# The heads' norm without reciprocals, the last combination in PSUM, the first keys queued ahead of the values' projection, the mLSTM's first loads off the queue of stores

## The chip, the core and the metric

The kernel runs on one core of a Trainium2 chip. The core has five engines that run side by side, each through its own list of instructions in order: PE (TensorE, matmuls and transposes), DVE (VectorE), ACT (ScalarE), POOL (GpSimd) and SP (SyncE, which issues most DMAs). The metric is the device time of one execution, in microseconds (us). The kernel before took 3703.52 us (median of three runs, 3697.98 to 3706.41).

## The reference

Two layers of a diffusion backbone over 1024 latent tokens and 256 context tokens, width 1024. A layer normalizes, projects, mixes by three groups of heads (a long convolution "hyena", an mLSTM, differential attention), projects back (`w_out`), routes each token to two of 32 experts, and adds up. What the change touches, cut:

```python
def diff_core(q, k, v, lam):                    # 4 heads, two maps m of 64 each
    s = einsum('bqhmd,bkhmd->bhmqk', q, k) * 64 ** -0.5
    pr = softmax(s, axis=-1)
    a = pr[:, :, 0] - lam * pr[:, :, 1]
    return einsum('bhqk,bkhe->bqhe', a, v)      # 128 wide

y_da = rmsnorm(o, da_subln_w) * (1 - lam_init)  # norm of each head's 128
rmsnorm(x, w) = x * rsqrt(mean(x * x) + 1e-6) * w
y = concat([y_hy, y_ml, y_da]) @ w_out          # x = x + g1 * y, norm, router
f = gate_0 * expert_0(h) + gate_1 * expert_1(h) # two experts per token
out = rmsnorm(x + g2 * f, final_norm_w)         # after the last layer
```

In layer 1 only the latent tokens are computed to the end; in layer 0 the 256 context tokens also attend, among themselves.

## The kernel before

Everything runs in stages, and each layer has the same ones: projections and hyena (with `da_v`, the projection of the attention's values, woven in; L329 stores them to `vD`), attention, the output stage `wout` (into which `ml_out`, the mLSTM's output, is woven), the experts. After layer 1's experts stands `final`.

**Attention** (`attention`, L1036 on) goes over 16 pairs of head and block of 256 queries, and in layer 0 over one more, the context (`None`). Its instructions stand on PE, DVE, ACT and POOL in an order that is written by hand: `AT_ORDER` (L1240) lists the steps of one iteration, in which pair i is scored, pair i-1 transposed and pair i-2 multiplied by the values. With x the half of 128 queries and m the map: `Sxm` are six matmuls of scores into one of two PSUM tiles `at_sc` (L1107); `Mxm` DVE's maximum over 1280 scores (L1113); `Exm` ACT's exponential, which also gives the row's sum (L1122); `Cx` (`comb`, L1127) makes c = -lambda * sum0 / sum1 on DVE (L1130, L1131), the reciprocal R = 1 / sum0 (L1132), and on POOL E1 * c (L1134) and E0 + E1 (L1138); `T`, `U`, `L` transpose on PE, copy the high part on ACT (L1161) and subtract for the low part on DVE (L1166). `O` and `Q` step the generator `out1` (L1169): value matmuls `at_av`, copy and square on ACT, the sum of squares by a matmul (`at_st`), then on DVE two multiplications by R (L1188, L1189), the mean (`rs_v`, L186), on POOL the power -1/2 (`rs_r`, L188), on DVE r * R (L1192), on PE its transpose `at_rb` (L1196), on DVE the product (L1198), on SP the store (L1199). `W` lets POOL round one piece of `w_out` (L1254). SP isn't in the hand-written order: a scheduler places its DMAs, each of which waits in line for those ahead of it, for its buffer, and for an earlier DMA of its ring of eight.

Queries have two buffers `at_q`, keys six `at_k` (four of them one head's). The context's queries lie in two `at_k`. The loads of an iteration stand in `prep` (L1044).

**The start of wout**: `ml_out(l, i)` loads five tiles for block i of 128 tokens (L925 to L932; in layer 0 the first two blocks from ACT's queue, the others from SP's) and computes `m_s` (scores), `m_o`, `m_i`, `m_p` on PE with exponentials and products between; `wout` (L1265) loads router weights `wr`, norm weights, `wo_x` and `wo_y` (the mixed heads), and multiplies `wo_o` by `w_out`. The router weights arrive with 4 and 32 numbers in a row of `wr`.

**The end**: `combine` (L1849) and `final` (L1891) take eight tiles of 128x1024: ACT gate0 * y0 (L1866), DVE + gate1 * y1 (L1867), POOL * g2 (L1868), DVE + x (L1869), ACT square and sum (L1900), DVE and POOL the inverse root, DVE x * r * w (L1902), store.

Of the kernel before, what the change touches and what calls it, by code (L numbers as in the profile page):

```python
# [8 lines left out]
F32 = mybir.dt.float32  # L9
# [20 lines left out]
class Kern:  # L30
# [885 lines left out]
    def ml_out(self, l, i, p, ps, psb):  # L916
# [6 lines left out]
        q = nc.scalar if i < 2 and l == 0 else nc.sync  # L923
# [112 lines left out]
    def attention(self, l, cx, p, pk, ps, psc, fill):  # L1036
# [5 lines left out]

        def prep(i):

            ctx = pairs[i] is None
            kt = lambda: pk.tile([128, 1280], F32R, name="at_k", bufs=6)
            vt = lambda: pk.tile([128, 10, 128], F32R, name="at_v", bufs=4)
            if ctx:
                kd = [[kt()[:, 0:1024].rearrange("p (h t) -> p h t", h=4) for y in range(2)] for m in range(2)]
# [11 lines left out]
                q = [kt()[:, 0:1024].rearrange("p (m h t) -> p m h t", m=2, h=4) for _ in range(2)]  # L1061
                for qi in range(2):
                    for m in range(2):
                        c = SEQ + qi * 128
                        for y in range(2):
                            nc.sync.dma_start(q[qi][64 * y:64 * y + 64, m].bitcast(F32),
                                              self.qkD[l][0, :, y, 64 * m:64 * m + 64, c:c + 128]
                                              .rearrange("h d t -> d h t"))
            else:
                h, qb = pairs[i]  # L1070
                q = pk.tile([128, 2, 256], F32R, name="at_q", bufs=2)
                for y in range(2):
                    nc.sync.dma_start(q[64 * y:64 * y + 64].bitcast(F32), self.qkD[l][0, h, y, :, qb * 256:(qb + 1) * 256]
                                      .rearrange("(m d) t -> d m t", m=2))
                if qb == 0:
                    kd = [[kt() for y in range(2)] for m in range(2)]
                    for m in range(2):
                        for y in range(2):
                            for x in range(2):
                                nc.sync.dma_start(kd[m][y][64 * x:64 * x + 64, :].bitcast(F32),  # L1080
                                                  self.qkD[l][1, h, y, 64 * m:64 * m + 64])
# [11 lines left out]

        def smm(i, x, m):
            u = st[i]
            w = u["nk"] * 128
            sc = u["sc"][x][m] = psc.tile([128, 1280], F32, name="at_sc", bufs=2)
            if u["ctx"]:
                for h in range(4):
# [1102 lines left out]
```

## Time and profile before

| | |
|---|---|
| time, three runs | 3697.98, 3703.52, 3706.41 us |
| the profiled execution: its own time, its span | 3701.92 us, 3700.1 us |
| mean granted TensorE clock | 0.924 of 2.4 GHz |
| busy: PE, DVE, ACT, POOL | 3214.9, 2553.5, 1726.5, 1175.7 us |
| layer 0: attention starts, ends | about 709, 978 us |
| layer 1: attention starts, ends | about 2543, 2801 us |
| the final combination | about 3643 to 3697 us |

The engines' busy shares (PE 87%, DVE 69%, ACT 47%, POOL 32%) are means over stages with different limits. A view of groups gives, for one line of the program, its instructions' total and mean; the idle time behind it is what the engine waited ahead of them and what ended the wait. In a view of a stretch in time, rows are in order and carry the idle time before them in brackets. A queue of DMAs ("SPq", "ACTq") shows when each issue began and how long it held the queue.

### The profile page before, as it was taken

How to read it: one execution, taken by the hardware profiler on the slowest of the kernel's cores; microseconds unless marked ns; L12 is line 12 of the kernel's file. 1: busy time of each engine (PE TensorE's matmuls, PEld its weight loads, DVE VectorE, ACT ScalarE, POOL GpSimd, SP SyncE). 2: the span in 40 equal slices, each digit the busy share in tenths (PEclk: the TensorE clock that was granted, in tenths of full speed). 3: DMA queues.
4: the chain of work that ended last, by engine and by line, in shares of the span. 5: the costliest groups of instructions: out<-in, count | busy, mean ns of one | idle time of the engine just before them, and what ended most of it. 6: DMA issues, size and time to landing. Idle time of an engine off the chain costs nothing. (4 is left out here: it accounts for less than half of the span.)

```text
span 3700.1 us, 48647 instructions
## 1 busy us (share of the span) xinstructions
PE 3214.9 (87%) x16486; PEld 2565.4 (69%) x16486; DVE 2553.5 (69%) x4367; ACT 1726.5 (47%) x2685; POOL 1175.7 (32%) x1101
## 2 busy tenths in 40 slices
PE   5999899888598898999997798987887989999992
PEld 2666777777577676677775687786776867777672
DVE  5444577488487687767676835875884877877776
ACT  3323233366332265556565423333663245666663
POOL 4000444277453212222110702442774411111104
PEclk7999899999798899999999799998998989999996
DMA  6889676543555677979797735776424578999985
GB/s 216 274 276 333 171 208 198 165 117 92 153 187 186 239 270 254 368 275 382 294 359 277 246 93 177 221 218 181 119 69 150 175 294 294 374 358 344 344 327 204
DMA packets 388509, 877.16 MB, mean 237 GB/s; under 512 B 60766, under 2 KB 244585, under 8 KB 332193
## 3 DMA queue, kind: packets, MB, share of 16 engines
q1 hardware_dynamic: 328945, 644.13, 51.8%
q10 hardware_dynamic: 25103, 145.74, 10.9%
q0 software_dynamic: 34208, 84.14, 7.2%
q8 instruction: 132, 2.16, 0.2%
q14 instruction: 121, 0.98, 0.1%
HBM read 750.32 MB, written 154.77 MB: 245 GB/s over the span
## 5 line engine op out<-in xcount | busy, mean ns | idle before, releaser
L1619 DVE TENSOR_TENSOR e_lo<-e_raw,e_hi 128x1024 fp32r<-128x1024 f32 x632 | 758.0, 1223 | 176.7 <-ACT e_hi L1618 168.4
L1618 ACT CAST e_hi<-e_raw 128x1024 fp32r<-128x1024 f32 x632 | 648.6, 1050 | 236.4 <-PE e_h L70 138.3
L68 PE MATMUL e_h<-e_hi,e_xh 128*128 128x512 f32 x768 | 328.8, 430 | 8.3 <-ACT e_hi L1618 8.2
L69 PE MATMUL e_h<-e_lo,e_xh 128*128 128x512 f32 x768 | 314.2, 409 | 2.3 <-DVE e_lo L1619 2.2
L70 PE MATMUL e_h<-e_hi,e_xl 128*128 128x512 f32 x768 | 300.9, 393 | 0.0
L68 PE MATMUL p_u<-hT,u_w 128*128 128x512 f32 (+1 forms) x768 | 290.7, 379 | 3.5 <-ACT u_w L60 3.5
L69 PE MATMUL p_u<-hT,u_w 128*128 128x512 f32 (+1 forms) x768 | 287.9, 375 | 0.0
L70 PE MATMUL p_u<-hT,u_w 128*128 128x512 f32 (+1 forms) x768 | 285.6, 373 | 0.0
L1600 PE MATMUL e_h<-e_raw,e_xf 128*128 128x512 f32 x512 | 249.6, 609 | 2.4 <-DVE e_sl L1611 2.2
L1653 POOL DMA_INDIRECT yD<-e_yo,rt_idx x66 | 88.3, 1338 | 479.2 <-ACT e_hi L1618 338.5
L1565 POOL DMA_INDIRECT e_xg<-h2D,rt_idx x66 | 84.2, 1276 | 488.3 <-PE e_tr L1581 352.6
L1122 ACT ACTIVATE at_e<-at_sc,at_S 128x1280 f32<-128x1280 f32 (+1 forms) x144 | 177.6, 1237 | 97.4 <-DVE at_S L1113 88.9
L1107 PE MATMUL at_sc<-at_k,at_q 128*128 128x512 f32 (+1 forms) x768 | 193.0, 388 | 32.2 <-DMA at_k<-qkD 23.5
L1113 DVE TENSOR_REDUCE at_S<-at_sc 128x1 f32<-128x1280 f32 (+1 forms) x132 | 194.1, 1472 | 33.7 <-PE at_sc L1107 28.6
L69 PE MATMUL e_y<-e_lo,e_hh 128*128 128x512 f32 x512 | 208.0, 410 | 1.4 <-DVE e_lo L1619 1.2
L70 PE MATMUL e_y<-e_hi,e_hl 128*128 128x512 f32 x512 | 193.0, 394 | 1.9 <-DVE e_hl L61 1.9
L1138 POOL TENSOR_TENSOR at_e<-at_e,at_e 128x1280 f32<-128x1280 f32 (+1 forms) x66 | 192.1, 2910 | 5.5
L68 PE MATMUL e_y<-e_hi,e_hh 128*128 128x512 f32 x512 | 181.6, 407 | 10.4 <-ACT e_hi L1618 8.0
L1107 PEld LDWEIGHTS at_sc<-at_k,at_q 128*128 128x128 f32 x768 | 143.1, 200 | 61.8 <-issue 23.3
L68 PEld LDWEIGHTS e_h<-e_hi,e_xh 128*128 128x128 f32 x768 | 145.2, 189 | 51.7 <-ACT e_hi L1618 17.8
L69 PEld LDWEIGHTS e_h<-e_lo,e_xh 128*128 128x128 f32 x768 | 145.0, 189 | 43.8 <-issue 11.4
L68 PEld LDWEIGHTS p_u<-hT,u_w 128*128 128x128 f32 x768 | 148.3, 193 | 35.6 <-issue 7.0
(576 smaller groups left out, 8287.9 us busy)
## 6 DMA issues: line engine op xcount, KB each, us to landing
e_raw<-in_moe_w_dram SPq DMA_DIRECT2D x259, 1024.0 KB
e_raw<-in_moe_w_dram ACTq DMA_DIRECT2D x121, 1024.0 KB
adaw<-in_ada_w_dram SPq DMA_DIRECT2D x48, 1024.0 KB
at_k<-qkD SPq DMA_DIRECT2D x64, 320.0 KB
u_raw<-in_w_in_dram SPq DMA_DIRECT2D x36, 512.0 KB
cb_y<-yD SPq DMA_DIRECT2D x36, 512.0 KB
hW<-in_c_hw_dram POOLq DMA_DIRECT2D x32, 512.0 KB, 4.9
at_v<-vD SPq DMA_DIRECT2D x16, 640.0 KB
```

The lines of the kernel that those rows point to most:

```text
L68: mm(out, L[0], R[0], start=start, stop=False)
L69: mm(out, L[0], R[1], start=False, stop=False)
L70: mm(out, L[1], R[0], start=False, stop=stop)
L1107: nc.tensor.matmul(sc[:, c:c + n], u["q"][:, m, x * 128:(x + 1) * 128], u["kd"][m][y][:, c:c + n], start=(y == 0), stop=(y == 1))
L1113: nc.vector.tensor_reduce(u["S"][x][:, m, 0:u["nh"]], sc[:, 0:w].rearrange("p (h t) -> p h t", h=u["nh"]), axis=AX.X, op=OP.max, negate=True)
L1122: nc.scalar.activation(e[:, cs], u["sc"][x][m][:, cs], AF.Exp, bias=S[:, m, h:h + 1], accum_out=S[:, 2 + m, h:h + 1])
L1138: nc.gpsimd.tensor_tensor(E[0], E[0], E[1], op=OP.add)
L1565: self.nc.gpsimd.indirect_dma_start(out=xg, out_offset=None, in_=self.h2D[l][0:NT, :], in_offset=bass.IndirectOffsetOnAxis(ap=gi, axis=0), ...
L1600: nc.tensor.matmul(hp[x], xx[0][:, k, :], raw[:, cs], start=(k == 0), stop=False)
L1618: self.nc.scalar.copy(hi, raw)
L1619: self.nc.vector.tensor_tensor(lo, raw, hi.bitcast(F32), op=OP.subtract)
L1653: u["o"].append(nc.gpsimd.indirect_dma_start(out=self.yD[l][0:2 * NT, :], out_offset=bass.IndirectOffsetOnAxis(ap=s, axis=0), in_=y, in_of ...
```

## The change

Six edits.

1. R is no longer a reciprocal. As E0 + E1 * c isn't divided by sum0, the norm can take EPS * sum0^2 in the place of EPS. `comb` computes that for both halves in one DVE instruction at C1 (L1149 of after) and drops both reciprocals; `out1` makes o / 128 + R in one instruction (L1205), POOL takes the power from it, and PE transposes that power directly: r * R (L1192) is gone, and one `Q` step.
2. `final` has its own loop: ACT writes gate0 * y0 into PSUM, three DVE instructions work there (+ gate1 * y1, * g2, + x), ACT squares from there; for six tiles ACT multiplies by r and POOL by w, for the last two DVE does both.
3. Queries have four buffers, and the context's queries lie in these, each loaded for itself ahead of its keys.
4. `first()` puts the first queries and keys ahead of those tiles of `da_v` that are emitted after hyena has ended (its memory is then free).
5. The mLSTM's loads all go by SP's queue; the attention's last two pairs store by POOL's queue; the exponentials `at_e` have a pool of their own, which is given back apart from the rest.
6. The router weights go through two contiguous tiles, and two DVE copies per layer.

```diff
@@ ml_out
-        q = nc.scalar if i < 2 and l == 0 else nc.sync
+        q = nc.sync
@@ attention: prep
+                q = [[qt().rearrange("p m (a t) -> p (m a) t", a=2) for m in range(2)] for _ in range(2)]
...
-                q = [kt()[:, 0:1024].rearrange("p (m h t) -> p m h t", m=2, h=4) for _ in range(2)]
-                q = pk.tile([128, 2, 256], F32R, name="at_q", bufs=2)
+                q = self.at_first[0] if i == 0 else self.at_queries(l, pk, h, qb)
                 if qb == 0:
-                    kd = [[kt() for y in range(2)] for m in range(2)]
+                    kd = self.at_first[1] if i == 0 else self.at_keys(l, pk, h)
@@ attention: comb, out1
             nc.vector.reciprocal(c, S[:, 3, 0:n])
             nc.vector.scalar_tensor_tensor(c, S[:, 2, 0:n], nlam, c, op0=OP.mult, op1=OP.mult)
-            nc.vector.reciprocal(u["R"][:, 0:n, x], S[:, 2, 0:n])
+            if x == 1:
+                s = u["S"][:, :, 2, 0:n].rearrange("p x h -> p h x")
+                nc.vector.scalar_tensor_tensor(u["R"][:, 0:n, :], s, EPS, s, op0=OP.mult, op1=OP.mult)
...
-            nc.vector.tensor_tensor(t, o[:, 0:2], R, op=OP.mult)
-            nc.vector.tensor_tensor(t, t, R, op=OP.mult)
-            r = self.rstd(p, t, 2, 1.0 / 128)
-            yield
-            nc.vector.tensor_tensor(R, r, R, op=OP.mult)
+            nc.vector.scalar_tensor_tensor(t, o[:, 0:2], 1.0 / 128, R, op0=OP.mult, op1=OP.add)
+            r = p.tile([128, 2], F32, name="rs_r", bufs=3)
+            nc.gpsimd.tensor_tensor(r, t, self.nhalf.to_broadcast([128, 2]), op=OP.pow)
...
-                nc.tensor.transpose(o[:, x * 128:(x + 1) * 128], R[:, x:x + 1].to_broadcast([128, 128]), self.ident)
+                nc.tensor.transpose(o[:, x * 128:(x + 1) * 128], r[:, x:x + 1].to_broadcast([128, 128]), self.ident)
...
-            nc.sync.dma_start(self.yTD[l][4 + h, :, u["qb"] * 256:(u["qb"] + 1) * 256], ob)
+            (nc.gpsimd if u["last"] else nc.sync).dma_start(self.yTD[l][4 + h, :, u["qb"] * 256:(u["qb"] + 1) * 256], ob)
...
-    AT_ORDER = """S00 O M00 T0 S01 T1 U0 O L0 E00 Q Q U1 M01 S10 T2 L1 E01 T3 O Q S11 U2 C0 O T4 M10 U3 E10 L2 L3
+    AT_ORDER = """S00 O M00 T0 S01 T1 U0 O L0 E00 Q U1 M01 S10 T2 L1 E01 T3 O Q S11 U2 C0 O T4 M10 U3 E10 L2 L3
@@ wout
+            wg = p.tile([128, 8, 4], F32, name="wr_g", tag="wo_h", bufs=2)
+            we = p.tile([128, 8, 32], F32, name="wr_e", tag="wo_h", bufs=2)
...
+            nc.vector.tensor_copy(wr[:, :, 0:4], wg)
+            nc.vector.tensor_copy(wr[:, :, 4:36], we)
@@ final
+                t = ps.tile([128, D], F32, name="fin_t", bufs=4)
+                nc.scalar.mul(t, y[0], self.gate[:, i, 0:1])
+                nc.vector.scalar_tensor_tensor(t, y[1], self.gate[:, i, 1:2], t, op0=OP.mult, op1=OP.add)
+                nc.vector.tensor_tensor(t, t, g2, op=OP.mult)
+                nc.vector.tensor_tensor(t, t, xt, op=OP.add)
+                nc.scalar.activation(sq, t, AF.Square, accum_out=ss)
+                r = self.rstd(p, ss, 1, 1.0 / D)
+                if i < 6:
+                    nc.scalar.mul(sq, t, r)
+                    nc.gpsimd.tensor_tensor(sq, sq, fw, op=OP.mult)
+                else:
+                    nc.vector.scalar_tensor_tensor(sq, t, r, fw, op0=OP.mult, op1=OP.mult)
@@ the layer
+                    def first():
+                        self.pk = cb.enter_context(pool(f"akv{l}", **right))
+                        self.at_first = self.at_queries(l, self.pk, 0, 0), self.at_keys(l, self.pk, 0)
...
                             with pool(f"wv{l}") as pw:
+                                if self.hyd:
+                                    first()
                                 yield from self.da_v(l, hT, pw)
...
+                pe = cb.enter_context(pool(f"ate{l}"))
```

DVE in a middle iteration of layer 0's attention, first before, from the sum of squares of one pair (`at_ms`) over C1 and M00 to the second subtraction; `at_A` are the subtractions L4, L0 and L1, `at_S` what belongs to the scores:

```order
L1188 TENSOR_TENSOR at_ms<-at_st,at_R 128x2
L1189 TENSOR_TENSOR at_ms<-at_ms,at_R 128x2
L186 TENSOR_SCALAR rs_v<-at_ms 128x2
L1166 TENSOR_TENSOR at_A_7598<-at_t,at_A_7597 128x512
L1130 RECIPROCAL at_S_7572<-at_S_7572 128x1
L1131 SCALAR_TENSOR_TENSOR at_S_7572<-at_S_7572,at_nl 128x1
L1132 RECIPROCAL at_R<-at_S_7572 128x1
L1113 TENSOR_REDUCE at_S_7719<-at_sc 128x1
L1166 TENSOR_TENSOR at_A_7746<-at_t,at_A_7745 128x4x128
L1192 TENSOR_TENSOR at_R<-rs_r,at_R 128x2
L1113 TENSOR_REDUCE at_S_7719<-at_sc 128x1
```

The same place on DVE of after:

```order
L1205 SCALAR_TENSOR_TENSOR at_ms<-at_st,at_R 128x2
L1183 TENSOR_TENSOR at_A_7555<-at_t,at_A_7554 128x512
L1145 RECIPROCAL at_S<-at_S 128x1
L1146 SCALAR_TENSOR_TENSOR at_S<-at_S,at_nl 128x1
L1149 SCALAR_TENSOR_TENSOR at_R<-at_S 128x2
L1128 TENSOR_REDUCE at_S<-at_sc 128x1
L1183 TENSOR_TENSOR at_A_7697<-at_t,at_A_7696 128x4x128
L1128 TENSOR_REDUCE at_S<-at_sc 128x1
```

Between the subtraction L0 and the maximum M01 nothing stands any more, three instructions for the mean are one, and behind C1's c stands the new product of the sums.

SP (the queue of loads and stores) at the end of layer 1's attention, before; `at_o` are the attention's stores, `ml_` the mLSTM's first block:

```order
L1199 DMA yTD_100<-at_o 128x256
L1252 DMA wo_raw<-in_w_out_dram 128x512
L1199 DMA yTD_100<-at_o 128x256 x3
L925 DMA ml_v<-vmD_90 128x260
L927 DMA ml_Cs<-CsD_98 128x260
L930 DMA ml_Mb<-mD_86 128x512 x2
L932 DMA ml_qk<-mqkD_92 128x4x128
```

The same place on SP of after:

```order
L1267 DMA wo_raw<-in_w_out_dram 128x512
L1214 DMA yTD_100<-at_o 128x256
L925 DMA ml_v<-vmD_90 128x260
L927 DMA ml_Cs<-CsD_98 128x260
L930 DMA ml_Mb<-mD_86 128x512 x2
L932 DMA ml_qk<-mqkD_92 128x4x128
```

The last two stores have left the queue (they are POOL's), so the mLSTM's loads stand behind the store of the last pair but two.

SP at the opening of layer 1's attention, before; `da_vl` and `da_vh` are stores of the projected values, two for each tile of 128 tokens and half of the columns, `hy_yo` one of hyena's:

```order
L691 DMA yTD_100<-hy_yo 128x1024
L329 DMA vD_94<-da_vh 128x256
L329 DMA vD_94<-da_vl 128x256
L1073 DMA at_q<-qkD_96 64x2x256 x2
L329 DMA vD_94<-da_vh 128x256
L329 DMA vD_94<-da_vl 128x256
L1080 DMA at_k<-qkD_96 64x1280 x8
L1084 DMA at_v<-vD_94 128x10x128 x2
```

The same place on SP of after:

```order
L691 DMA yTD_100<-hy_yo 128x1024
L329 DMA vD_94<-da_vh 128x256
L329 DMA vD_94<-da_vl 128x256
L1045 DMA at_q<-qkD_96 64x2x256 x2
L1054 DMA at_k<-qkD_96 64x1280 x8
L329 DMA vD_94<-da_vh 128x256
L329 DMA vD_94<-da_vl 128x256
L329 DMA vD_94<-da_vh 128x256
L329 DMA vD_94<-da_vl 128x256
L1099 DMA at_v<-vD_94 128x10x128 x2
```

Four stores of values stand behind the first keys now, where none stood.

## Rows read from the trace of the kernel before

**Rows 1.** Stretches: PE, PEld, DVE, ACT, POOL busy; clock; DMA share; GB/s

```profile
725.00:925.00 200.00, 167.51 (x1106) 148.79 (x1105) 177.21 (x273) 131.33 (x222) 146.72 (x84) 0.97 0.39 101
978.20:1005.30 27.10, 7.27 (x41) 6.33 (x41) 5.68 (x21) 6.50 (x18) 5.86 (x5) 0.50 0.98 312
2801.00:2827.00 26.00, 7.34 (x40) 6.33 (x40) 6.71 (x26) 6.48 (x18) 6.50 (x6) 0.53 0.87 266
3643.00:3697.00 54.00, 0.00 (x0) 0.00 (x0) 42.56 (x32) 17.83 (x24) 34.86 (x16) 0.50 0.62 248
```

**Rows 2.** Waits, 725 to 925 us: total, times, longest

```profile
PE at_rb L1196 <- DVE at_A L1166: 19.9, 11, 2.1
PE at_sc L1107 <- DMA at_k<-qkD: 5.0, 3, 2.2
```

**Rows 3.** DVE in order of time, one iteration: start, duration, idle before

```profile
805.10 2.56 DVE L1192 TENSOR_TENSOR at_R<-rs_r,at_R 128x2 f32<-128x2 f32 x1
...
810.80 0.22 DVE L1131 SCALAR_TENSOR_TENSOR at_S<-at_S,at_nl 128x1 f32<-128x1 f32 x1
...
811.34 1.49 DVE L1113 TENSOR_REDUCE at_S<-at_sc 128x1 f32<-128x1280 f32 x1 [0.25 <-PE at_sc L1107]
...
817.31 0.15 DVE L1132 RECIPROCAL at_R<-at_S 128x1 f32<-128x1 f32 x1
...
819.42 2.48 DVE L1192 TENSOR_TENSOR at_R<-rs_r,at_R 128x2 f32<-128x2 f32 x1
```

**Rows 4.** POOL in order of time, the same iteration

```profile
817.56 1.33 POOL L1134 TENSOR_SCALAR at_e<-at_e,at_S 128x1280 f32<-128x1280 f32 x1 [0.89 <-DVE at_R L1132]
818.98 2.90 POOL L1138 TENSOR_TENSOR at_e<-at_e,at_e 128x1280 f32<-128x1280 f32 x1
821.84 1.29 POOL L1254 TENSOR_TENSOR wo<-wo_raw,wo 128x512 fp32r<-128x512 f32 x1
```

**Rows 5.** Groups by line, 725 to 925 us: busy, mean ns

```profile
L1192 DVE TENSOR_TENSOR at_R<-rs_r,at_R 128x2 f32<-128x2 f32 x13 | 32.5, 2497 | 0.0
L1188 DVE TENSOR_TENSOR at_ms<-at_st,at_R 128x2 f32<-128x2 f32 x13 | 1.9, 148 | 0.0
```

**Rows 6.** One line in layer 1, 2590 to 2775 us: shortest, median, longest

```profile
L1192 DVE TENSOR_TENSOR at_R<-rs_r,at_R x13: 2489/2507/2544, 2596.9 to 2771.3; 128x2 f32<-128x2 f32 x13
```

**Rows 7.** PE's waits, 930 to 950 us (the context pair)

```profile
PE at_sc L1101 <- DMA at_k<-qkD: 5.6, 1, 5.6
```

**Rows 8.** PE's waits, 2540 to 2580 us (layer 1's opening)

```profile
PE at_sc L1107 <- DMA at_k<-qkD: 13.2, 4, 8.0
```

**Rows 9.** SP's queue at that opening: start, time held

```profile
2545.26 4.97 SPq L1080 DMA_DIRECT2D at_k<-qkD  x8
```

**Rows 10.** ACT's and SP's queues at the two starts of wout

```profile
976.71 9.93 ACTq L930 DMA_DIRECT2D ml_Mb<-mD  x2
986.76 0.41 ACTq L932 DMA_DIRECT2D ml_qk<-mqkD  x1
...
2790.40 11.17 SPq L1199 DMA_DIRECT2D yTD<-at_o  x3
```

**Rows 11.** PE's waits, 978 to 1006 us, then 2800 to 2920 us

```profile
PE m_s L937 <- DMA ml_qk<-mqkD: 16.2, 1, 16.2
...
PE m_s L937 <- DMA ml_qk<-mqkD: 7.6, 1, 7.6
PE wo_o L68 <- ACT wo_yh L60: 7.2, 1, 7.2
```

**Rows 12.** Groups by line, 3643 to 3700 us: busy, mean ns

```profile
L1902 DVE SCALAR_TENSOR_TENSOR n_sq<-e_raw,rs_r 128x1024 f32<-128x1024 f32 x6 | 16.0, 2667 | 0.0
L1867 DVE SCALAR_TENSOR_TENSOR cb_y<-cb_y,gate,cb_y 128x1024 f32<-128x1024 f32 x8 | 15.3, 1917 | 11.6 <-DMA cb_y<-yD 11.6
L1869 DVE TENSOR_TENSOR e_raw<-e_raw,cb_y 128x1024 f32<-128x1024 f32 x6 | 7.2, 1208 | 0.0
L1902 DVE SCALAR_TENSOR_TENSOR n_sq<-cb_x,rs_r,e_raw 128x1024 f32<-128x1024 f32 x2 | 2.6, 1281 | 0.7 <-POOL rs_r L188 0.7
```

More of the change, by code (lines that the diff above doesn't have):

```diff
@@ L1034, in at_consts, with at_kt, at_qt, at_queries @@
         nc.vector.tensor_scalar(sub, self.vcol("sub"), 1.0 - li, None, op0=OP.mult)
-    def attention(self, l, cx, p, pk, ps, psc, fill):
+    def at_kt(self, pk):
+        return pk.tile([128, 1280], F32R, name="at_k", bufs=6)
+    def at_qt(self, pk):
+        return pk.tile([128, 2, 256], F32R, name="at_q", bufs=4)
+    def at_queries(self, l, pk, h, qb):
+        q = self.at_qt(pk)
+        for y in range(2):
+            self.nc.sync.dma_start(q[64 * y:64 * y + 64].bitcast(F32), self.qkD[l][0, h, y, :, qb * 256:(qb + 1) * 256]
+                                   .rearrange("(m d) t -> d m t", m=2))
+        return q
+    def at_keys(self, l, pk, h):
+        kd = [[self.at_kt(pk) for y in range(2)] for m in range(2)]
+        for m in range(2):
+            for y in range(2):
+                for x in range(2):
+                    self.nc.sync.dma_start(kd[m][y][64 * x:64 * x + 64, :].bitcast(F32),
+                                           self.qkD[l][1, h, y, 64 * m:64 * m + 64])
+        return kd
+    def attention(self, l, cx, p, pe, pk, ps, psc, fill):
         tc, nc, I = self.tc, self.nc, self.I
@@ L1088, in prep @@
             nh = 4 if ctx else 1
-            st[i] = dict(ctx=ctx, kd=kd, v=v, q=q, nh=nh, nk=8 if ctx else 10, E=[[None, None], [None, None]],
+            st[i] = dict(last=i >= N - 2, ctx=ctx, kd=kd, v=v, q=q, nh=nh, nk=8 if ctx else 10, E=[[None, None], [None, None]],
                          sc=[[None, None], [None, None]], t={},
                          R=p.tile([128, 4, 2], F32, name="at_R", bufs=4),
-                         S=[p.tile([128, 5, 4], F32, name=f"at_S{x}", bufs=2) for x in range(2)])
+                         S=p.tile([128, 2, 5, 4], F32, name="at_S", bufs=2))
         def smm(i, x, m):
@@ L1117, in sexp @@
             u = st[i]
[L1118 to L1119 removed]
+            w, S, g = u["nk"] * 128, u["S"][:, x], u["nk"] * 128 // u["nh"]
+            e = u["E"][x][m] = pe.tile([128, 1280], F32, name=f"at_e{m}", bufs=2 if m else 4)[:, 0:w]
             for h in range(u["nh"]):
```

86 lines of the change are left out of this document (41 added, 45 removed).

## The prediction

> **What bounds the kernel now.** I read the stretches first [rows 1]. In layer 0's attention (725 to 925 us) PE is busy 167.5 of 200 us and DVE 177.2, so neither is quite the bound; at the two starts of `wout` (978 to 1005, 2801 to 2827 us) PE is busy 7.3 us of 27 and 26, at half its clock; in the last 54 us PE does nothing and DVE 42.6 us. So the change is worth what it takes from a wait in those three places. I then read the waits, the engines' rows in time, and the queues.
>
> In the attention the largest wait of PE is ahead of `at_rb`: 19.9 us in 11 waits, about 1.8 each [rows 2]. It has its cause on DVE: r * R, a product of 128x2 numbers, takes 2.48 us at 819.42 [rows 3], and the sum E0 + E1 on POOL (818.98, 2.90 us) ends at 821.88, just when it ends [rows 4]. 13 such products take 32.5 us [rows 5], 13 more in layer 1 have a median of 2.507 [rows 6]. A product with one input in PSUM, of the same size, takes 0.148 us [rows 5]. So DVE's small product with both inputs in SBUF stands still while POOL adds, and the maximum M01, its exponential and PE's `at_rb` stand behind it.
>
> The Trainium skill ("SBUF — State Buffer", section "Who interferes with whom") says the same: DVE and POOL share one pair of SBUF ports, a DVE instruction with two SBUF inputs and a POOL instruction that reads SBUF exclude each other, and the later one waits for the whole of the other. The rows above agree. It speaks for taking out L1192, but the new product of sums (L1149) has two SBUF inputs as well, and that is a rival below.
>
> **1. The attention.** One iteration lasts 14.32 us (805.10 to 819.42, [rows 3]). The change takes L1192 out of it, 2.48 us on the path M00, L0, R, M01. All three instructions for the mean become one with a PSUM input; the two that go, some 0.15 each [rows 5], stand ahead of a wait of C1 for its exponential, so I count them at nothing (0.3 each iteration if that wait were gone). Against it: M01's and L1's inputs from ACT come closer together, which I estimate at 0.18 us; and C0's c (0.22 us at 810.80, two SBUF inputs) moves nearer to POOL's rounding of `w_out` (1.29 us at 821.84 [rows 4], one iteration on), which may hold it for some tenths, of which the 0.25 us that M10 waits for PE anyway [rows 3] hide about half: another 0.25. That leaves 2.05 us. Is there room? PE is busy 83.8% of the stretch [rows 1], 12.0 us of 14.32 by share, and part of that is its pipelined matmuls' modelled ends; POOL's 73% are 10.5 us; DVE's 88.6% are 12.7, of which 2.35 are the standing still (2.497 - 0.148). A period of 12.27 us just holds all of these, PE most tightly. The bounds are then 0.7 (below, first rival) and 2.35.
>
> Of 13 long products in each layer, three stand where the head changes: there PE waits for `at_k`, 5.0 us in three waits [rows 2], for loads that start only when the last scores of the head before have given up their buffers. Their start moves with the iteration, their flight doesn't, so I take 0.5 us there (bounds 0 and 2.05). Sum: 20 x 2.05 + 6 x 0.5 = **44 us**, bounds 14 and 53.
>
> **2. The context pair and the tails.** PE waits 5.6 us for the context's tiles [rows 7], since its queries lie in two `at_k` that must first come free. With `at_q` of their own the first ones are early; the last key and the last queries still come late. I take **4 us** (bounds 1 and 5.6). At both ends of the attention the norm's chain runs without cover; five times three DVE instructions of 0.15 us [rows 5] fall out of it: **2 us** (0 to 4, with their handovers).
>
> **3. Layer 1's opening.** PE waits 13.2 us in four waits for the first keys [rows 8]; these are issued in 4.97 us from 2545.26 [rows 9]. In the new order they stand four stores of values earlier, before the last two tiles of `da_v` rather than behind them: about as long as two of PE's tiles, some 4 us. The loads' own flight remains, and they now fly beside those stores. **3 us** (0 to 4). In layer 0 there is no such wait, and I count nothing; the values' stores now stand behind the keys, but `at_v` is needed an iteration later than the keys, which covers it.
>
> **4. The two starts of wout.** In layer 0 `m_s` waits 16.2 us for `ml_qk` [rows 11]: it is issued only at 986.76, since `ml_Mb` ahead of it held ACT's queue 9.93 us from 976.71 on [rows 10]. In layer 1 it waits 7.6 us, with SP's queue held 11.17 us from 2790.40 by three stores of the attention, and then `wo_o` waits 7.2 us for `wo_yh` [rows 10, 11]. After the change the last two stores are off SP's queue, the loads wait for buffers that come free an iteration earlier, and the data lie ready when attention ends. What is late next is the mLSTM's own chain: its scores, exponentials and products on four engines, in which PE has little to do, and on PE `wo_o` now stands behind the second block's `m_o` and the first's `m_p` instead of in front of them. On SP the loads of `wo_x` and `wo_y` now stand behind the third block's `ml_v` and `ml_Mb`, which wait for PE to have used the first block's. So I don't take the sum of the waits, 16.2 and 14.8, but 9 and 8: **17 us** together (bounds 3 and 27; the upper one leaves 2 us of each start to the chain).
>
> The Trainium skill ("DMA: Bandwidth & Descriptors", section "Issuing engines are not separate DMA queues") speaks against this step: DMAs from all queues run on the same 16 DMA engines, and using several queues saves only the time to issue. DMA's share is 0.98 and 0.87 in these stretches [rows 1], which fits it; but the rows of the queues show loads that weren't issued at all. By the page the term would be near nothing: the second rival.
>
> The small pieces: contiguous router weights take short packets off the queue; the two copies on DVE are small; neither is on the path after the wait above, and they are in its bounds.
>
> **5. The end.** DVE sets the pace: eight of L1867 (1917 ns), eight of L1869 (1208), six of L1902 at 2667 and two at 1281 [rows 12]: 15.3 + 9.7 + 16.0 + 2.6 = 43.6 us. The 2667 and 1917 are again longer than the 1281 of the same form where POOL is idle. After: for each tile one of 1.28 and two of 1.21 with an operand in PSUM, plus two of 1.28 at the end: 8 x 3.70 + 2.6 = 32.2. PSUM operands cost about the same by the maxima's 1.49 us for 1280 numbers [rows 3]. That is 11.4 less; 1.4 go to a start in which DVE now waits for ACT's first product. ACT has four passes for six tiles, POOL's product by w and its power lie beside: **10 us** (5 to 12).
>
> **The sum.** 44 + 4 + 2 + 3 + 17 + 10 = 80 us from the profiled execution's 3701.92 gives 3622 us; the median of the runs is 1.6 higher, which is no matter here.
>
> **The rivals.** *The standing still moves.* C1's new product (two SBUF inputs) comes right behind c at the place where the old reciprocal began at 817.31, and POOL's scaling by c starts at 817.56 [rows 3, 4]. Today the DVE instruction is first by 0.25 us. If POOL is first, M00 waits for 1.33 us in each of 20 iterations: 27 us back, **3649 us**. By the page on SBUF both would wait in whole instructions, as here. *The loads gain nothing*, because transfers and not queues set both starts, or because the chain and `wo_y` take the place of the wait: 17 and the 3 of the opening fall away, **3642 us**. That the loads don't move forward as they should, being held for other buffers, gives the same. *All of it comes off*: 2.3 in an iteration, 12 and 11 at the starts, 4 at the opening: 80 + 5 + 6 + 1 + 2 = 94 gives **3608 us**. *Slower*: with a period near 12 us POOL's 10.5 us leave few gaps, and each small DVE instruction with two SBUF inputs (C0's c, C1's c, the new product) can meet a long one: 1.29 + 2.90 + 1.33 = 5.5 us in an iteration in place of 2.48. It decides from 3.4 us on: beyond 2.05, 26 times 1.4 use up the other 36 us. At 5.5 the time would be 3702 - 36 + 26 x 3.45 = about **3756 us**. Against it: c of C1 waits for an exponential that ends after that sum.
>
> **How the numbers follow.** The forecast 0.55, the standing still moved 0.15, no gain from loads 0.13, all of it 0.12, slower 0.02, little change by several of these together 0.03. The range holds the first four: 3602 to 3652 us. A difference under 0.2% (7 us) can't be told from no change. Faster by more 0.95, within it 0.03, slower 0.02.
>
> **What would show it.** Right: the iteration's spacing at 12.2 to 12.4 us, no DVE instruction of 128x2 above 1 us, PE's wait for `at_rb` nearly gone; `m_s` without a wait for a DMA; DVE's period at the end 3.7 to 4 us. Wrong: L1149 or C0's c with means above 0.5 us, a wait of PE for `at_k` that grows by as much as `at_rb` loses, a `wo_o` that starts 25 us behind the attention's end as before.

## The result, and the profile after

The changed kernel took 3607.28 us (median of four runs, 3603.48 to 3611.38), beside 3703.11 us of the kernel before (median of four): a ratio of 0.9745 with a 95% interval of 0.9728 to 0.9761, 96 us less. The forecast was 3622 us, 80 us less, in a range of 3602 to 3652. The profiled execution took 3603.48 us, its span is 3601.7 us, 98.4 shorter than before's.

Where these 98.4 us lie is read by cutting both spans at the same landmarks: the first and the last start of one instruction on PE (or the first load of y on SP). All numbers are worked out from such starts.

| stretch | before | after | difference |
|---|---|---|---|
| to hyena's last transposes, layer 0 | 639.0 | 642.6 | +3.6 |
| from there to the first scores, layer 0 | 70.3 | 74.3 | +4.0 |
| scores of 16 pairs, layer 0 | 220.0 | 197.3 | -22.7 |
| context pair and tail, to the last `at_rb` | 47.9 | 42.0 | -5.9 |
| last `at_rb` to the first `m_s` | 16.6 | 0.3 | -16.3 |
| first `m_s` to the last router matmul | 259.2 | 259.2 | 0.0 |
| layer 0's experts | 768.2 | 768.0 | -0.2 |
| layer 1's opening, to its first scores | 529.6 | 518.3 | -11.3 |
| scores of 16 pairs, layer 1 | 228.4 | 204.5 | -23.9 |
| tail, to the last `at_rb` | 21.2 | 22.1 | +0.9 |
| last `at_rb` to the first `m_s` | 7.9 | 0.2 | -7.7 |
| first `m_s` to the last router matmul | 174.5 | 170.3 | -4.2 |
| layer 1's experts | 660.8 | 659.1 | -1.7 |
| the end, from the first load of y | 56.5 | 43.5 | -13.0 |

How far such a row can be trusted is seen from pairs of executions of one program, below: stretches of 200 us and more differ by up to 6 us (layer 1's scores once by 8), the short ones by 1 or 2.

The stretches of after that answer to [rows 1] (columns as there: PE, PEld, DVE, ACT, POOL busy, granted clock, DMA share, GB/s):

```profile
730.00:912.00 182.00, 167.03 (x1126) 149.02 (x1125) 144.60 (x227) 135.88 (x229) 149.27 (x85) 0.99 0.44 112
956.00:980.40 24.40, 14.61 (x77) 12.20 (x77) 11.86 (x43) 9.97 (x28) 15.00 (x16) 0.50 0.96 313
2728.00:2751.00 23.00, 12.82 (x69) 11.01 (x70) 11.13 (x31) 9.75 (x28) 13.49 (x14) 0.55 0.79 241
3558.00:3601.00 43.00, 0.00 (x0) 0.00 (x0) 31.21 (x34) 23.66 (x30) 18.29 (x14) 0.50 0.81 318
```

In the attention PE has gone from 84% to 92% busy and is the engine nearest to a bound now. From the attention's end to the first `wo_o` PE is busy 14.6 and 12.8 us, where it was 7.3: the time is hardly shorter (24.2 us after the last `at_rb` instead of 28.1 in layer 0), but it is filled. The data are there: the first block's `ml_qk`, which answers to [rows 10] and in layer 0 was issued 9.6 us after the attention's last `at_rb`, is issued 12.7 us ahead of it in layer 0 and 8.8 us in layer 1 (SP's queue: start, time held):

```profile
943.47 0.38 SPq L932 DMA_DIRECT2D ml_qk<-mqkD  x1
...
2719.79 0.43 SPq L932 DMA_DIRECT2D ml_qk<-mqkD  x1
```

DVE in order of time, one iteration of after, which answers to [rows 3] (start, duration):

```profile
804.17 0.22 DVE L1146 SCALAR_TENSOR_TENSOR at_S<-at_S,at_nl 128x1 f32<-128x1 f32 x1
804.30 0.15 DVE L1149 SCALAR_TENSOR_TENSOR at_R<-at_S 128x2 f32<-128x2 f32 x1
...
809.88 0.31 DVE L1146 SCALAR_TENSOR_TENSOR at_S<-at_S,at_nl 128x1 f32<-128x1 f32 x1
...
816.29 0.22 DVE L1146 SCALAR_TENSOR_TENSOR at_S<-at_S,at_nl 128x1 f32<-128x1 f32 x1
...
820.83 1.49 DVE L1128 TENSOR_REDUCE at_S<-at_sc 128x1 f32<-128x1280 f32 x1 [2.20 <-PE at_sc L1122]
```

and POOL in the same iteration, which answers to [rows 4]:

```profile
804.56 1.34 POOL L1151 TENSOR_SCALAR at_e<-at_e,at_S 128x1280 f32<-128x1280 f32 x1 [1.28 <-DVE at_R L1149]
...
808.87 1.30 POOL L1269 TENSOR_TENSOR wo<-wo_raw,wo 128x512 fp32r<-128x512 f32 x1
```

From one C1 to the next it is 12.12 us (804.17 to 816.29), where it was 14.32. The new product (L1149) takes 0.15 us and is ahead of POOL's scaling by 0.26 us; POOL's row names it as what it waited for. The c of C0 (809.88) takes 0.31 us instead of 0.22: it ends at 810.19, when POOL's rounding (808.87 + 1.30) has ended. At the change of head, the maximum at 820.83 waits 2.20 us for PE, which waits for keys. The waits of after from 730 to 912 us, of those of [rows 2] only the second is left (total, times, longest):

```profile
PE at_t L1167 <- DVE at_A L1183: 6.4, 12, 1.6
PE at_sc L1122 <- DMA at_k<-qkD: 6.0, 3, 2.2
```

### The profile page after: what moved, and what is told of

Read it like the earlier page. It is cut to its first block, busy times and chain, and to the rows that moved or that the text cites. A ratio compares the mean times of both kernels' runs of the same rounds, so it can differ in the third digit from the quotient of the medians.

```text
span 3601.7 us, 48555 instructions
## 1 busy us (share of the span) xinstructions
PE 3196.9 (89%) x16486; PEld 2553.0 (71%) x16486; DVE 2471.0 (69%) x4232; ACT 1732.2 (48%) x2691; POOL 1172.2 (33%) x1106
## 4 chain that ended last, share of the span: by engine, by line
PE 40%; DVE 8%; DMA 6%; issue 5%; ACT 3%; POOL 3%; SPq 1%; POOLq 0%; DVEq 0%; ACTq 0%
PE e_h L1619 6%; PE e_h L69 4%; PE e_h L70 4%; PE e_h L68 4%; PE e_y L68 3%; PE e_y L70 3%; PE e_y L69 3%; PE e_tr L1600 1%; ACT e_hi L1637 1%; DVE e_lo L1638 1%; PE p_u L69 1%; PE p_u L68 1%; DMA at_k<-qkD 1%; PE p_u L70 1%; DVE at_S L1128 1%
## 5 line engine op out<-in xcount | busy, mean ns | idle before, releaser
L68 PE MATMUL e_y<-e_hi,e_hh 128*128 128x512 f32 x512 | 181.6, 407 | 10.5 <-ACT e_hi L1637 8.0
L69 PEld LDWEIGHTS e_h<-e_lo,e_xh 128*128 128x128 f32 x768 | 144.9, 189 | 42.2 <-issue 11.1
```

What stands on the lines that cost most here:

```text
L68: mm(out, L[0], R[0], start=start, stop=False)
L69: mm(out, L[0], R[1], start=False, stop=False)
```

## The experiments

Twelve kernels were run. Each is the kernel before or the changed one with the edit shown. Ratios are against runs of the kernel before in the same job. Edit 3 (the queries' buffers) and edit 6 (the router weights) were not run by themselves.

### The standing still, tested alone

```diff
-            nc.vector.tensor_tensor(R, r, R, op=OP.mult)
+            for x in range(2):
+                nc.vector.tensor_scalar(R[:, x:x + 1], R[:, x:x + 1], r[:, x:x + 1], None, op0=OP.mult)
```

> The kernel before with one edit: r * R (L1192, 128x2, two inputs in SBUF) as two multiplications of 128x1 by a scalar per partition, so that each has one tensor input. Nothing else changes, the reciprocals and the chain stay. Theory of the standing still (an instruction of DVE with two inputs in SBUF waits while POOL adds): both take some 0.15 to 0.2 us, 26 iterations get 2.1 us shorter, less at the changes of head: 3655 to 3665 us. Rival (it waits for POOL's power, for POOL's queue or for a handover, whatever its form): the first of the two is as long as before, 3700 to 3706 us.

Measured: 3667.3 us, ratio 0.9919 (0.9899 to 0.9940), 31 us less, just above the 3655 to 3665 expected. The group of the line in layer 0's attention of this run (busy, mean ns; answers to [rows 5]):

```profile
L1193 DVE TENSOR_SCALAR at_R<-at_R,rs_r 128x1 f32<-128x1 f32 x26 | 4.2, 203 | 0.0
```

The same product of the same numbers at the same place takes 0.2 us twice instead of 2.5 us, beside the same sums on POOL. What made it wait was its second tensor input, and neither POOL's power nor a handover: the rival is out. Both attentions are as short as the changed kernel's (first to last score, context included: 214.1 and 206.3 us, there 214.1 and 204.5, before 240.1 and 228.4), 48 us less. That the whole gained less is the third thing to be seen here (38.5 us from span to span; the four executions of this kernel lie between 3661 and 3674 us): layer 0's output stage takes 8.3 us more from its first `m_s` (267.5 instead of 259.2) and layer 0's experts 4 more, though the edit doesn't touch them. The order of the instructions in these stages is another than before: the scheduler places the rest of the program anew when one instruction changes. How much of the 12 us is that order, and how much the 5 us by which such stages also differ in one program, isn't shown.

### The norm alone

The kernel before with edit 1.

> The kernel before with edit 1 alone (the norm without reciprocals, one Q less). If the gain of the attention is this edit's, both attentions lose 23 us each as in the changed kernel, and the tails some 3: 3650 to 3658 us. If it needs the other edits (more buffers for queries, early keys): 3665 to 3690. The difference to the run with one input (same wait removed, more instructions) should be 2 to 8 us.

Measured: 3648.54 us, ratio 0.9861 (0.9844 to 0.9877), 50 us less, a little more than expected. Scores take 214.2 and 205.7 us. So the attention's gain is this edit's alone, and nearly all of it is the wait of the run above; the shorter chain shows in the tails (25.4 and 19.2 us, before 27.8 and 21.2). The run is 19 us faster than the one with one input, where 2 to 8 were expected. From span to span it is 9.9 us: 4 in the tails and 5 in layer 1's opening, which the edit doesn't touch.

### The end alone

The kernel before with edit 2.

> The kernel before with edit 2 alone (the last combination in PSUM). In the changed kernel the stretch from the first load of y to the end is 13.0 us shorter. If that is this edit's: 3689 to 3692 us. Rival: part of the 13 is the state in which the experts' stage leaves the queues, then 3692 to 3698.

Measured: 3685.06 us, ratio 0.9962 (0.9948 to 0.9977), 13 us less than this job's kernel before (3698.12 us), and the stretch itself is 42.2 us instead of 56.5. The gain is the edit's; which part of it is PSUM's and which the new division among ACT, POOL and DVE, no run separates. Up to there this is the same program as the kernel before, in the same order, so it shows how stages repeat: layer 1's opening 526.1 and 529.6 us, layer 0's output stage from `m_s` 263.8 and 259.2.

### The loads alone

The kernel before with edits 5 and 6.

> The kernel before with edits 5 and 6 alone (mLSTM's loads on SP, last stores on POOL, a pool of their own for the exponentials, contiguous router weights). From the end of attention to the last router matmul the changed kernel is 16.3 and 11.9 us shorter. If these edits do it by themselves: 3673 to 3679 us. If it came from data that land earlier only since attention is shorter, or if the 16 DMA engines set the start whatever the queue: 3695 to 3706.

Measured: 3692.57 us, ratio 0.9984 (0.9971 to 0.9996), 6 us less. PE's waits for `m_s` are gone here too (0.4 us from the last `at_rb` in both layers), but in layer 0 the stage from `m_s` on takes 270.3 us instead of 259.2 and gives 11 of the 16 us back. In layer 1 it is 170.1 instead of 174.5, so all of it stays. Together the two stages are 17 us shorter, but the profiled execution only 7.3: layer 0's experts take 8.3 us more (776.5 instead of 768.2), and other stretches the rest. Both expectations missed. The edits do free the start by themselves; what follows it depends on the order that the scheduler finds.

The three parts alone gain 50, 13 and 6 us, 69 of the 96. The other 27 came only with all six together.

### The last stores on SP again, and one pool again

In the changed kernel:

```diff
-            (nc.gpsimd if u["last"] else nc.sync).dma_start(self.yTD[l][4 + h, :, u["qb"] * 256:(u["qb"] + 1) * 256], ob)
+            nc.sync.dma_start(self.yTD[l][4 + h, :, u["qb"] * 256:(u["qb"] + 1) * 256], ob)
```

> The changed kernel with the attention's last stores back on SP's queue; the loads of the mLSTM stay there too. Theory: the queue is held by the stores until attention ends, m_s waits again, and PE has nothing under the chain: 12 to 25 us for both starts, 3619 to 3632. Rival: what counts is that loads no longer wait for the exponentials' buffers, then 3607 to 3612.

Measured: 3642.92 us, ratio 0.9846 (0.9805 to 0.9886), by the ratios 37 us more than the changed kernel (0.0101 of 3703). SP's queue at the end of layer 0's attention (start, time held):

```profile
948.93 0.43 SPq L927 DMA_DIRECT2D ml_Cs<-CsD  x1
949.63 1.42 SPq L1214 DMA_DIRECT2D yTD<-at_o  x2
951.10 1.44 SPq L930 DMA_DIRECT2D ml_Mb<-mD  x2
952.98 0.37 SPq L932 DMA_DIRECT2D ml_qk<-mqkD  x1
```

Loads stand behind stores again: the second block's `ml_qk` is issued 3.3 us after the last `at_rb`, in the changed kernel 9.6 us ahead of it. From the last `at_rb` to the last router matmul both output stages take 34 us more together (278.6 instead of 259.5, 185.1 instead of 170.5). That is more than the 12 to 25 expected, and most of it isn't the wait that the theory named. The first `m_s` waits 2.9 and 4.0 us for its data; 26 of the 34 us lie behind it. In layer 0 the longest of PE's waits there is for the second block's product on DVE, and DVE had the norm's weights in front of it in line, a load from the same queue (PE's waits from 945 to 1010 us; DVE in order of time):

```profile
PE m_o L950 <- DVE ml_Mb L946: 10.5, 1, 10.5
...
971.77 1.23 DVE L1321 SCALAR_TENSOR_TENSOR wo_sc<-wo_sc,wo_n 128x1024 f32<-128x1024 f32 x1 [8.49 <-DMA wo_sc<-modD]
```

The order of the stage is another than the changed kernel's, too; what is the late loads' and what the order's, this run doesn't separate.

And the exponentials in the attention's pool:

```diff
-                pe = cb.enter_context(pool(f"ate{l}"))
+                pe = pa
```

> The changed kernel with the exponentials in the attention's pool again (given back with the rest of it). Theory: the mLSTM's first tiles lie where tiles of the last pair were and wait for its end, so m_s waits some 7 us in each layer: 3615 to 3625. Rival: the stores on the queue were what held the loads: 3606 to 3610.

Measured: 3651.85 us, ratio 0.9868 (0.9826 to 0.9910), 45 us more than the changed kernel. PE waits in this run, 940 to 1000 us:

```profile
PE m_s L937 <- DMA ml_qk<-mqkD: 12.8, 1, 12.8
```

So both are needed in this kernel: buffers that come free early, and a queue on which nothing stands in front. Each of the two losses is larger than expected. In the second run the wait for `m_s` is 13.2 and 4.6 us from the last `at_rb` (16.6 and 7.9 in the kernel before), and both output stages take 36 us more together; 12 more lie in layer 1's opening, which is 530.4 us here. That PE also lacks the data for the later blocks' steps fits the 10.5 us above, but isn't shown for all of it.

### The first keys

In the changed kernel, once with the early keys in layer 1 alone, once in no layer:

```diff
-                                if self.hyd:
+                                if self.hyd and l:
```

```diff
-                                if self.hyd:
+                                if False:
```

> The changed kernel, but with the first keys ahead of the values' projection in layer 1 alone; layer 0 loads them as before. Theory: in layer 0 eight keys' loads stand ahead of the values' stores, the projection's buffers come free late and PE waits 7 us: without that 3600 to 3604 us (the changed kernel has 3607). Rival: the 7.6 us by which layer 0's attention starts later come from elsewhere in the opening, then 3605 to 3609.

> The changed kernel with the first keys behind the values' projection in both layers. If the early keys gain 3 to 5 us in layer 1 and cost 4 to 7 in layer 0: 3602 to 3608, and 3 to 5 above the run with layer 1 alone. If all of the 11 us by which layer 1's opening got shorter are theirs: 3610 to 3614.

Measured: 3620.88 us (ratio 0.9779, 0.9738 to 0.9820) and 3618.57 us (0.9777, 0.9737 to 0.9817). Both expectations missed, and the reason is plain from the program: instruction for instruction the two are the same. In layer 1 `self.hyd` is still false when the values' projection begins, so `first()` isn't taken there but only after the projection, as without edit 4; the early keys are layer 0's alone. The four stores behind the first keys that the order of after shows in layer 1 are thus the scheduler's and not this edit's. The two runs are one program twice (experts of layer 0 774.1 and 769.0 us, layer 1's opening 532.3 and 538.0).

In layer 0 the early keys do cost what their place suggests. PE's waits of after from 638 to 722 us:

```profile
PE p_n L68 <- DVE da_v L324: 10.2, 2, 7.0
PE at_sc L1122 <- ACT at_e L1137: 1.9, 1, 1.9
PE p_n L68 <- ACT wv L60: 1.7, 2, 1.0
```

Before had 8.4 us for `wv` there and no wait of the projection for `da_v`. DVE waited in turn for a store to free its buffer, and that store stood on SP's queue behind the eight keys (656.31 to 662.16 us); without the early keys the longest such wait was 1.9 us. Of after:

```profile
671.23 0.43 DVE L61 TENSOR_TENSOR da_vl<-da_v,da_vh 128x256 fp32r<-128x256 f32 x1 [13.47 <-DMA vD<-da_vl]
```

From hyena's end to the first scores five executions with before's loads took 69.6 to 70.6 us, these two 73.3 and 71.1, and seven with the early keys 72.5 to 74.7. So 2 to 4 us are lost in layer 0; the whole is nevertheless 12 us faster with them, and that difference lies in layer 1's opening.

### What layer 1's opening depends on

Fourteen executions fall into groups. Of after, PE's waits from 2494 to 2530 us, and of the run with seven buffers of keys (below) from 2480 to 2530 us:

```profile
PE at_sc L1122 <- DMA at_k<-qkD: 9.7, 4, 4.9
PE at_sc L1122 <- ACT at_e L1137: 2.3, 3, 0.9
```

```profile
PE at_sc L1124 <- DMA at_k<-qkD: 16.2, 4, 11.1
PE f_p L68 <- ACT f_hi L60: 1.9, 3, 1.3
```

The keys' memory comes free when hyena ends. In after hyena's transposes end 8.5 us before the values' projection (504.6 and 513.1 us after the first load of y), so that the projection covers part of the time that the keys take; in the other run hyena ends last (523.2 and 521.5), nothing covers it, and PE waits 11.1 us at once. Before lies between (515.6, 521.3, a wait of 8.0 us, [rows 8]). But from hyena's end to the first scores it is 13.9 us before, 13.7 in after and 11.4 in the other run, and 11.1 to 14.0 in all fourteen executions: the first scores follow hyena, however long PE's wait is. All programs with hyena last took 529 to 538 us for the opening (the runs with one input, with one pool, the two above and two below), those with hyena 6 us ahead 524 to 530, those with 8 us ahead 518 to 522. The order of the two is the scheduler's, and it changed with edits that have nothing to do with it. Of the 11.3 us, 11.0 are thus hyena's earlier end (515.6 to 504.6); PE's shorter wait (8.0 to 4.9) isn't a gain beside it. Why hyena ends earlier in that order, no run takes apart.

A kernel that is the changed one up to the end shows that the opening belongs to the program and not to chance:

```diff
-                if i < 6:
+                if i < 7:
                     nc.scalar.mul(sq, t, r)
```

> The changed kernel with seven tiles instead of six in which ACT multiplies by r and POOL by w in the final stage. All that is ahead of the final stage is the same program as the changed kernel's, so its stages show how well a stage repeats: if layer 1's opening (from the first load of y to the first score) is 516 to 521 us again, its 11 us are the order's; if 525 to 532, chance. The final stage itself: DVE has 1.3 us less, POOL's product of 2.35 us stands at the end instead: 42.5 to 45 us (43.5 in the changed kernel), within 2 us of the changed kernel as a whole.

Measured: 3603.75 us, ratio 0.9734 (0.9707 to 0.9761), which can't be told from the changed kernel's 0.9745. Layer 1's opening is 517.7 us: the order's. The end takes 46.2 us, 2.7 more and above the 42.5 to 45 expected, so six tiles were the better choice. Layer 1's scores took 212.5 us in this execution, 8 more than after's, in the same program. The granted clock differs; from 2500 to 2710 us of this run, and from 2505 to 2715 us of after:

```profile
2500.00:2710.00 210.00, 190.38 (x1196) 169.50 (x1197) 157.25 (x245) 146.84 (x246) 161.60 (x92) 0.92 0.45 111
```

```profile
2505.00:2715.00 210.00, 187.25 (x1210) 164.81 (x1211) 159.34 (x247) 148.84 (x249) 164.42 (x93) 0.95 0.47 117
```

### wo_x and wo_y from ACT's queue

In the changed kernel, for the first block of each layer:

```diff
+                    qy = nc.scalar if i == 0 else nc.sync
-                    self.dmae().dma_start(xt, src)
+                    (nc.scalar if i == 0 else self.dmae()).dma_start(xt, src)
-                    nc.sync.dma_start(yt[:, 0:2, :], self.yTD[l][0:2, :, ts].rearrange("k p t -> p k t"))
+                    qy.dma_start(yt[:, 0:2, :], self.yTD[l][0:2, :, ts].rearrange("k p t -> p k t"))
-                    nc.sync.dma_start(yt[:, 2:6, :], self.yTD[l][4:8, :, ts].rearrange("k p t -> p k t"))
+                    qy.dma_start(yt[:, 2:6, :], self.yTD[l][4:8, :, ts].rearrange("k p t -> p k t"))
```

> The changed kernel with the first block's wo_x and wo_y loaded from ACT's queue in both layers, so that they don't stand behind the third block's mLSTM loads on SP. Theory: the start of wout is late by that queue, wo_o then begins 5 to 10 us earlier after the attention's end in each layer (24 and 22 us in the changed kernel), and half of that is kept, as PE had other work in it: 5 to 10 us less. Rival: the chain of the mLSTM and the 16 DMA engines (share 0.96 there) set it: within 3 us of the changed kernel.

Measured: 3627.97 us, ratio 0.9800 (0.9775 to 0.9824), 20 us more than the changed kernel, where 5 to 10 less were expected. `wo_o` does begin earlier, 4.4 and 10.4 us (19.5 and 11.6 us after `m_s`, where it was 23.9 and 22.0). But from there to the last router matmul it takes 18.6 and 11.6 us more, so that the stage is 14.2 longer in layer 0 and 1.2 in layer 1; besides, layer 1's opening has its long form (534.6 us). PE's waits of this run, 950 to 1010 us, show the new one:

```profile
PE wo_o L68 <- ACT wo_yh L60: 6.5, 1, 6.5
PE m_o L950 <- issue: 4.8, 2, 3.1
```

So the earlier `wo_o` gained nothing here. In after PE did the mLSTM's steps of the next blocks ahead of it, and these are then not in the way later; as this run's order is another in the whole stage, that is the likely reason, and not shown.

### c with one tensor input

In the changed kernel, for the pairs with one head:

```diff
+            if n == 1:
+                nc.vector.tensor_scalar(c, c, nlam, S[:, 2, 0:1], op0=OP.mult, op1=OP.mult)
+            else:
-            nc.vector.scalar_tensor_tensor(c, S[:, 2, 0:n], nlam, c, op0=OP.mult, op1=OP.mult)
+                nc.vector.scalar_tensor_tensor(c, S[:, 2, 0:n], nlam, c, op0=OP.mult, op1=OP.mult)
```

> The changed kernel with c = -lambda * sum0 / sum1 as one multiplication by two scalars per partition (one tensor input in SBUF instead of two). Theory of the shared ports: C0's c, which stands still until POOL's rounding of w_out ends (0.31 us, up to 0.585), takes 0.2 us always; 0.1 to 0.3 us in each of 32 iterations, of which M10's wait for PE hides half: 1 to 5 us less than the changed kernel. Rival: the iteration is set by PE and by C1's exponential, then nothing.

Measured: 3603.24 us, ratio 0.9733 (0.9709 to 0.9756): not to be told from the changed kernel. The two forms of c in layer 0's attention (shortest, median, longest ns), first the changed kernel's, then this run's:

```profile
L1146 DVE SCALAR_TENSOR_TENSOR at_S<-at_S,at_nl x28: 218/220/585, 727.6 to 899.8; 128x1 f32<-128x1 f32 x28
```

```profile
L1147 DVE TENSOR_SCALAR at_S<-at_S,at_nl x32: 272/273/276, 717.8 to 913.6; 128x1 f32<-128x1 f32 x32
```

With one tensor input it never waits, but with its two scalars it takes 0.05 us more than the undisturbed other form, each time. Neither shows in the time. That is what the rival said; that PE sets the iteration now is the likely reason (92% busy).

### Seven buffers of keys

The run with one-input c, and:

```diff
-        return pk.tile([128, 1280], F32R, name="at_k", bufs=6)
+        return pk.tile([128, 1280], F32R, name="at_k", bufs=7)
-        return pk.tile([128, 2, 256], F32R, name="at_q", bufs=4)
+        return pk.tile([128, 2, 256], F32R, name="at_q", bufs=2)
```

with the second half of the context's queries in a buffer of keys.

> The changed kernel with c as in the run with one input, seven buffers of keys instead of six and two of queries instead of four (half of the context's queries in a buffer of keys, as before). At a change of head two loads of keys instead of four then wait for the last scores of the head before. Theory: PE's three waits of 2 us for keys in each layer, which r * R used to hide half, shrink to under 1 us each: each layer's scores 3 to 5 us shorter (about 210 and 200 us in place of 214 and 204), the context's loads some 2 us later. As the order of the other stages is placed anew, layer 1's opening may be 518 or 530 us: 3594 to 3614 in all, and only the scores tell. Rival: the wait is the flight of whatever is loaded last: scores unchanged.

Measured: 3605.33 us, ratio 0.9737 (0.9717 to 0.9757). The scores are 8.8 and 5.6 us shorter (205.3 with the context, and 198.9 us), more than the 3 to 5 expected, and PE's waits from 725 to 905 us have no key among them:

```profile
PE at_t L1172 <- DVE at_A L1188: 6.0, 15, 0.8
PE at_sc L1124 <- ACT at_e L1139: 0.2, 1, 0.2
PE at_t L1172 <- POOL at_e L1160: 0.2, 1, 0.2
```

So the head changes' wait of after (6.0 us in a layer) was real and could be had; what the other 3 us in layer 0 are isn't shown. But layer 1's opening came out in its long form (534.6 us instead of 518.3), which is all of it and 2 us more. It doesn't beat the changed kernel; a version that keeps both wasn't found here.

## Why the prediction was right, and where it wasn't

**1, the attention: 44 us forecast, 46.6 measured.** The step held as it was worked out: 14.32 to 12.12 us in an iteration is 2.2, forecast 2.05. The held c at C0 came as foreseen and cost 0.09 us in the iteration shown, where 0.25 was allowed. The head changes stayed as waits of 2 us for keys, as foreseen. The first rival, the standing still at the new product, didn't come: L1149 stayed ahead of POOL's scaling by 0.26 us and took 0.15. How exact the 46.6 is, the other execution of this program shows: there layer 1's scores took 8 us more. One bound of the sum was wrong: with 2.35 us in each iteration the upper one is 59 and not 53, which is 26 times 2.05. The Trainium skill's rule ("SBUF — State Buffer", section "Who interferes with whom") agrees with the run with one input: the same product with one tensor input takes 0.203 us beside POOL's sum.

**2, context pair and tails: 6 forecast, 5.0 measured** (5.9 less in layer 0, 0.9 more in layer 1). The context's first scores follow the last pair's after 1.4 us instead of 7.3, but take 15.4 us instead of 12.8, as the late tiles that were foreseen hold them (a wait of 3.0 us for `at_k`).

**3, layer 1's opening: 3 forecast, 11.3 measured, and for another reason.** The step took the four stores behind the keys for the work of `first()`; in layer 1 it isn't called there, as the two runs without a difference show. What stood there was the scheduler's order of hyena and projection. PE's longest wait did shrink by 3.1 us, the size forecast, but that is luck: the time from hyena's end to the first scores stayed (13.9 and 13.7 us), so the shorter wait gained nothing by itself. And the step that counted nothing for layer 0 failed: "`at_v` is needed an iteration later than the keys, which covers it". What wasn't covered is that the stores free the projection's own buffers, so DVE waits 13.5 us for a store and PE for `da_v`. The stretch cost 4.0 us; the 3.6 ahead of it lie in the same program before and after, which took 635.9 to 642.6 us over fourteen executions, so they are no effect.

**4, the starts of wout: 17 forecast, 28.2 measured.** This is the term that was mis-sized. It took the waits of 16.2 and 7.6 us as replaced in part by the mLSTM's chain, "what is late next". But the chain stood behind the wait before, too: from the first `m_s` to the last router matmul the stage lasts 259.2 us before and 259.2 after. So the whole wait ahead of `m_s` was gain, 16.3 + 7.7 = 24.0, and 4.2 came from behind it in layer 1. That layer 0's two numbers are equal is partly chance. Two executions of the program before have 259.2 and 263.8, two of after's 259.2 and 255.2; and the run with the loads alone, with the same waits gone, has 270.3 and so gives 11 us back, which fits the forecast's 9 for a start better than the 16. The full gain is thus measured for this kernel and not for the edits as such.

The foreseen order (`wo_o` behind the second block's steps, `wo_y` behind the third block's loads) did come. By the sign named for being wrong, a `wo_o` 25 us behind the attention's end, the term would have failed: it starts 24.2 and 22.2 us after the last `at_rb`, before 28.1 and 26.6. The sign was badly chosen, as PE works in that time now. The second rival, that queues don't matter, fell with the run with the loads alone, where the waits for `m_s` are gone (0.4 us) though the same data are moved, and with the stores back on SP the time is 37 us more. The Trainium skill ("DMA: Bandwidth & Descriptors", section "Issuing engines are not separate DMA queues") says that several queues save only the time to issue. The measurement differs here: in layer 0 the two `ml_Mb` held ACT's queue 9.93 us [rows 10], and the load behind them wasn't issued for as long.

**5, the end: 10 forecast, 13.0 measured.** DVE's eight products with gate1 take 1283 ns each, eight and eight others 1227 and 1229, as forecast. None stands still any more, as those of 1917 and 2667 did; DVE's busy time fell by 11.4 us (42.56 to 31.21), which is the sum's 43.6 - 32.2 (answers to [rows 12]; busy, mean ns):

```profile
L1925 DVE SCALAR_TENSOR_TENSOR fin_t<-cb_y,gate,fin_t 128x1024 f32<-128x1024 f32 x8 | 10.3, 1283 | 10.7 <-DMA cb_y<-yD 10.7
L1926 DVE TENSOR_TENSOR fin_t<-fin_t,e_raw 128x1024 f32<-128x1024 f32 x8 | 9.8, 1227 | 0.0
L1927 DVE TENSOR_TENSOR fin_t<-fin_t,e_raw 128x1024 f32<-128x1024 f32 x6 | 7.4, 1228 | 0.0
L1927 DVE TENSOR_TENSOR fin_t<-fin_t,cb_x 128x1024 f32<-128x1024 f32 x2 | 2.5, 1233 | 0.0
L1936 DVE SCALAR_TENSOR_TENSOR n_sq<-fin_t,rs_r,e_raw 128x1024 f32<-128x1024 f32 x2 | 2.6, 1278 | 1.4 <-POOL rs_r L188 1.4
```

The start was only 0.4 us later (DVE's first product 5.6 us after the first load, before 5.2), where 1.4 had been taken off, and POOL's power no longer waits (552 ns, before 1245 in the same stretch).

The forecast's total was short by 16 us on the medians and by 18 on the spans (98.4 for 80): 11 for term 4, 8 for layer 1's opening, 3 for the end, 3 for the attention, 2 for the experts, less 8 for layer 0's opening and 1 for the tails. The time came out where the rival "all of it comes off" stood, 3608. It had 23 us for the starts, 2.3 for an iteration and 4 for the opening; 28.2, 2.2 and 11.3 were measured. That the total meets it is luck in part: 8 us of it are the opening's order, which no edit was made for, and about as much was lost in layer 0's opening.

Open is why hyena ended earlier in layer 1, beyond that the order did it.

## What to carry to other kernels

A tiny instruction that takes as long as another engine's large one, and ends when it ends, is standing still and not working: give it another form of operands before moving it. A wait for data at the start of a stage can be worth its full length when the chain behind it was already behind it; what takes the wait's place must be taken off, and here that hung on the order that the scheduler found (all 16 us kept in one kernel, 5 in another). Where a scheduler places the program, compare stage by stage and run one program twice: a gain in one stage was in part paid back in another that the edit doesn't touch (17 us gained, 7 kept, in the run with the loads alone).

## What the runs showed of the hardware

A DVE multiplication of 128x2 numbers with both inputs in SBUF took 2.26 to 2.57 us beside a sum of 128x1280 on POOL, and 0.203 us for each half when the second input was a scalar per partition. A multiplication of 128x1 with two scalars per partition took 0.273 us, against 0.220 for the form with two tensors when nothing was in its way. ACT's 128x1024 product took 1118 ns into PSUM (1138 into SBUF before, mean of eight each), and its square 1023 ns from PSUM (1057 from SBUF). One program (up to its last stage), executed twice, had a granted clock of 0.95 and 0.92 in about the same 210 us, and layer 1's scores took 8 us more at 0.92.
